# Router on the residual itself, routing in four batches, row numbers ahead of the weight splits, an early empty gather

## The chip, the core and the metric

One core of a Trainium2 chip runs the whole kernel. The metric is the device time of one execution in microseconds, the median of three runs. Five engines work from queues of their own: TensorE (PE; its weight loads are PEld), VectorE (DVE), ScalarE (ACT), GpSimd (POOL) and SyncE (SP, which here only issues transfers). DMA transfers are issued by SP, ACT and POOL.

## The reference

One layer on 1024 tokens of 1024 channels, float32. Only the last two residual steps are touched.

```python
x = x + mixed @ w_out
x = x + memory_cross_attention(x, mem, ...)          # 4 heads, 256 memory tokens
x = x + hierarchical_moe(rms_norm(x, norm_ffn), ...)

def rms_norm(x, g):
    return x * lax.rsqrt(jnp.mean(x * x, axis=-1, keepdims=True) + EPS) * g

def hierarchical_moe(hf, ...):                       # 4 groups x 8 experts
    gval, gidx = lax.top_k(softmax(hf @ w_group + b_group), 1)
    el = take_group(hf @ w_router + b_router, gidx)  # 8 logits of the chosen group
    ev, eidx = lax.top_k(el, 2)
    ew = softmax(ev) * gval
    # each expert: rows of hf sent to it, (silu(x @ w_g) * (x @ w_u)) @ w_down, times ew, added to out
```

## The kernel before, in words

Tokens come in 8 blocks of 128 (tb = 0 to 7). The kernel runs, in time: RMSNorm and the q, k, v and gate projections, differential attention, the RG-LRU, the merge and w_out, which leaves the residual in the tiles x1 (one per block); then the memory attention with the router, and last the 32 experts.

Every weight comes through the class `Weights` as pieces of 128 x 1024 floats (512 KB) that SP loads ahead. Each is split exactly into two parts of a shorter float format: ACT writes `wh` (L90), DVE writes `wl` (L94). Every product of large matrices is three matmuls on such parts (L152 to L154, `mm3`); `split` (L320, L321) does the same with activations, ACT first and then DVE. SBUF tiles come from one pool of 4-KB slots, so an instruction may also wait until the former holder of its slot is done. `prefetch` (op f) lets the stream run ahead by PF[i] pieces.

Between w_out and the experts, a string SEQ gives the order in which the steps are written. A letter is a step, a digit the block (or pair of blocks g):

- A, P, T, S: norm, query projection, its transposes, scores and softmax. O, M: transposes of the probabilities, product with the memory values (tile `om`, split by ACT, then DVE).
- C: product with w_co into `pco` (24 matmuls of 512 columns). It reads `om`.
- N (`st_N`): x1 += pco (DVE, L1007), squares with their sum (ACT, L1008), store of x1 to the output (issued by ACT, L1009), the row factor r = rstd on POOL (L1012 to L1014), then h3 = x1 * r * gain (DVE, L1018; tile `n`) and its store to DRAM, `h3_d` (issued by ACT, L1020). For blocks 6 and 7 the steps of N go in two halves.
- R (`st_R`): 8 transposes of h3 on PE (`ph3T`, L1033), split into `h3T`.
- L (`st_L`): router logits of a pair of blocks, 16 matmuls with the router weights as the stationary side (`plog`, 72 rows: a high and a low part of 36 logits, 256 tokens, L1045); bias and copy by ACT (`lgT`, L1049). l (`st_l`): transposes back and sum of the parts (`plgT`, L1055), copied by DVE (L1056).
- r and q (`st_route`): its first half chooses group and experts (some 25 small DVE operations, L1125 to L1143), its second half counts the rank of each token in its expert with matmuls (`prk`, L1147 to L1150) and builds one-hots (`ohs`, `vals`, L1167 and L1176). Batches are blocks 0-1, 2-3 and 4 to 7.

After SEQ, matmuls `pTi` and `pTw` (L1262) collect token numbers and weights per expert slot; DVE turns them into `idx` and `wts` (L1270 to L1272). POOL's indirect gather fetches the 96 rows of h3 of an expert from `h3_d` (tile `xe`, L1282); PE transposes them (`pxe`, L1292), and `pgu` begins the expert. An instruction scheduler orders each engine's queue within these steps; queues run in order.

Of the kernel before, what the change touches and what calls it, by code (L numbers as in the profile page):

```python
# [124 lines left out]
def block_kernel(ctx, tc, a):  # L125
# [301 lines left out]
    # --------------------------------------------------- differential attention  # L427
# [3 lines left out]
    def head_load(h):  # L431
        """Per map: q stacks its two parts on the partitions, k repeats each part."""
# [66 lines left out]
    def w_transpose(h, g):  # L499
        """Transposes of the query pair g; parts per two key blocks: [128 keys, 2, 256 queries]."""  # L500
# [141 lines left out]
    # ------------------------------------------------------------------ RG-LRU  # L642
# [17 lines left out]
    V.scalar_tensor_tensor(t5, t5, 2.0, t0, op0=OP.mult, op1=OP.add)   # softplus(-lam)  # L660
# [48 lines left out]
    def lru_gate(c):  # L709
        """2 * gelu of the gate."""  # L710
# [12 lines left out]
    def lru_scan(c):  # L723
        """Block-diagonal gates, recurrence, times the gate."""
# [25 lines left out]
    # memory keys and values  # L750
# [87 lines left out]
    # --------------------------------- attention output, gated: 2 * sigmoid(g) * y  # L838
# [12 lines left out]
    # -------------------------------------------------- LRU output, merge, w_out  # L851
# [22 lines left out]
    # ------------------------------------------- memory attention, MoE input  # L874
# [9 lines left out]
    nc.sync.dma_start(wr, a["w_r"])  # L884
    A.activation(wrs[:, :, 0:36], wr, AF.Copy)
# [9 lines left out]
    def pair_T(src, kp, name):  # L895
        """Channels 256 * kp ... of two token blocks: parts [128 channels, 2 parts, 2, 256 tokens]."""
# [104 lines left out]
    def st_N(tb, ps):  # L1001
# [19 lines left out]
        x1[tb] = None  # L1021

    h3T, lgT = {}, {}

    def st_R(tb):
        """Transposes of a token block for the router: parts [128 channels, 4, 256 tokens]."""
        src = h3.pop(tb)
        c = slice((tb % 2) * P, (tb % 2) * P + P)
        for kq in range(2):
            ps = bank(f"ph3T{tb}_{kq}", F32, (P, 4, P))  # L1030
# [3 lines left out]
            if tb % 2 == 0:  # L1034
                h3T[tb // 2, kq] = [slot(f"h3T{tb}_{kq}_{i}", F32R, (P, 4, 256)) for i in range(2)]
            t = h3T[tb // 2, kq]
            split(ps, t[0][:, :, c], t[1][:, :, c])

    def st_L(g):
        """Router logits of two token blocks: [36 high and 36 low parts, 256 tokens]."""  # L1040
        pl = bank(f"plog{g}", F32, (P, 256))[0:72]
# [9 lines left out]
    def st_l(g):
        src = lgT.pop(g)
        pt = bank(f"plgT{g}", F32, (P, 2, 36))
        for j in range(2):
# [34 lines left out]
    lgf = rt("lg", NB * 36)  # L1089
# [3 lines left out]
    id2 = rt("id2", 36)[0:72]  # L1093
    V.tensor_tensor(id2, ident[0:72, 0:36], ident[0:72, 36:72], op=OP.add)
    coded = []

    def st_route(b0, n2):
        """Choices of n2 token blocks, then their ranks within the experts and dispatch codes."""
# [14 lines left out]
        def first_hot(v, mxv, n):  # L1113
            """One-hot of the first maximum along the last axis."""
# [37 lines left out]
        # weights of the two choices  # L1152
        V.tensor_reduce(sg, gd, axis=AX.X, op=OP.add)
        V.reciprocal(gval, sg)
        V.tensor_tensor(m2, m2, m1, op=OP.subtract)
        A.activation(m2, m2, AF.Exp)
        V.tensor_scalar(dn, m2, 1.0, None, op0=OP.add)
        V.reciprocal(dn, dn)
        V.tensor_tensor(ew[:, 0, bs], dn, gval, op=OP.mult)
        V.tensor_tensor(ew[:, 1, bs], ew[:, 0, bs], m2, op=OP.mult)  # L1160
        V.tensor_copy(ewh[:, :, bs], ew[:, :, bs])
        V.tensor_tensor(ewl[:, :, bs], ew[:, :, bs], f(ewh[:, :, bs]), op=OP.subtract)
# [43 lines left out]
    PF = 12,20,28,36,41  # L1206
    SEQ = ("P0 T0 P1 T1 S0 S1 P2 P3 O00 O01 O02 T2 O03 T3 M00 M01 C0 A2 S2 S3 N0 C1 N1 P4 O10 O11 P5 "
# [3 lines left out]
    done = set()  # L1211
    routes = [st_route(0, 2), st_route(2, 2), st_route(4, 4)]
    pco = {}
    for op in SEQ.split():
# [29 lines left out]
        elif kind == "l":  # L1244
            st_l(n)
# [10 lines left out]
    def b3(ap, n):      # [P, NB] -> [P, NB, n]  # L1256
# [246 lines left out]
```

## Time and profile before

| what | value |
|---|---|
| median of 3 runs | 1965.66 us (1961.47, 1965.66, 1966.36) |
| profiled execution: span from first to last instruction | 1957.1 us |
| lowest run less that span | 4.4 us |
| median less that span | 8.6 us |
| PE busy | 1882.8 us, 96% |
| PEld, DVE, ACT, POOL busy | 79%, 66%, 56%, 17% |
| mean granted clock of TensorE | 0.988 |

The profiled execution is one of its own; only its span is known, and 4.4 to 8.6 us lie around it if it was like the timed runs. Busy shares are means over stages with different limits, so the stage that a change touches has to be read by itself. A row of the timeline gives the start, the duration (of the whole group if xN), engine, line, operation, output<-inputs, shapes, and in brackets the engine's idle time just before and what ended it.

### The profile page before, as it was taken

To read this page: it belongs to the slowest core of one execution; us is meant where nothing else is said; L and a number is where in the kernel's file an instruction comes from. 1 tells how busy PE (TensorE), PEld (TensorE's weight loads), DVE (VectorE), ACT (ScalarE), POOL (GpSimd) and SP (SyncE) were. 2 spreads that over 40 slices of the span, in tenths; PEclk is the share of its full clock that TensorE was granted. 3 is DMA by queue.
4 is the path that set the end of the run, shared out by engine and by line. 5 is a ranking of instruction groups with operands and counts; after the bars stand their busy time and mean duration, and the time that the engine had idled before them with its cause. 6 is when DMAs were issued, how large, how long until landed. Compare 5 with 4: busy or idle time off the path is not lost. (4 is left out here: it accounts for less than half of the span.)

```text
span 1957.1 us, 27981 instructions
## 1 busy us (share of the span) xinstructions
PE 1882.8 (96%) x10366; PEld 1551.2 (79%) x10366; DVE 1295.3 (66%) x1766; ACT 1087.6 (56%) x1607; POOL 337.1 (17%) x430
## 2 busy tenths in 40 slices
PE   7999999999999999989999999996999999999996
PEld 7999998888888888867888888885777777777664
DVE  5222233777778767887534434776899999999985
ACT  5222223555555545875412214543788888888885
POOL 2343251122222221110000000211111111111110
PEclk9999999999999999989999999998999999999998
DMA  4222225433334322214422511167999999999996
GB/s 167 98 80 94 87 87 152 133 99 115 96 108 120 107 81 79 82 51 173 150 67 84 197 33 65 54 248 296 297 340 361 345 349 360 340 354 342 352 368 217
DMA packets 103130, 353.53 MB, mean 181 GB/s; under 512 B 14224, under 2 KB 15376, under 8 KB 102992
## 3 DMA queue, kind: packets, MB, share of 16 engines
q1 hardware_dynamic: 91088, 322.10, 46.7%
q0 software_dynamic: 7296, 17.04, 3.8%
q10 hardware_dynamic: 4608, 12.58, 1.6%
q8 instruction: 82, 1.34, 0.3%
q14 instruction: 56, 0.46, 0.1%
HBM read 311.82 MB, written 48.23 MB: 184 GB/s over the span
## 5 line engine op out<-in xcount | busy, mean ns | idle before, releaser
L94 DVE TENSOR_TENSOR wl<-wraw,wh 128x1024 fp32r<-128x1024 f32 x480 | 578.4, 1230 | 104.2 <-ACT wh L90 91.9
L90 ACT ACTIVATE wh<-wraw 128x1024 fp32r<-128x1024 f32 x480 | 496.4, 1057 | 111.3 <-DVE wl L94 18.3
L153 PE MATMUL pgu<-wl,xeh 128*96 128x512 f32 x512 | 203.5, 397 | 1.2 <-DVE wl L94 1.0
L152 PE MATMUL pgu<-wh,xeh 128*96 128x512 f32 x512 | 203.4, 397 | 0.3 <-ACT wh L90 0.3
L154 PE MATMUL pgu<-wh,xel 128*96 128x512 f32 x512 | 200.9, 392 | 0.0
L486 ACT ACTIVATE p<-pS,st 128x256 f32<-128x256 f32 (+7 forms) x128 | 94.9, 747 | 93.7 <-DVE st L479 53.2
L154 PE MATMUL pqk<-wh,hL 128*128 128x256 f32 x512 | 145.2, 284 | 0.0
L153 PE MATMUL pqk<-wl,hH 128*128 128x256 f32 x512 | 145.1, 283 | 0.0
L152 PE MATMUL pqk<-wh,hH 128*128 128x256 f32 x512 | 145.0, 283 | 0.0
L152 PE MATMUL pga<-hH,wh 128*128 128x512 f32 x320 | 127.8, 399 | 3.5 <-DVE wT L520 3.5
L153 PE MATMUL pga<-hL,wh 128*128 128x512 f32 x320 | 126.3, 395 | 0.0
L154 PE MATMUL pga<-hH,wl 128*128 128x512 f32 x320 | 125.9, 393 | 0.0
L153 PEld LDWEIGHTS pgu<-wl,xeh 128*96 128x96 f32 x512 | 82.8, 162 | 44.0 <-DVE wl L94 13.0
L152 PEld LDWEIGHTS pgu<-wh,xeh 128*96 128x96 f32 x512 | 82.8, 162 | 33.8 <-ACT wh L90 0.5
L154 PEld LDWEIGHTS pgu<-wh,xel 128*96 128x96 f32 x512 | 82.8, 162 | 33.1 <-DVE xel L321 0.2
L1332 POOL DMA_INDIRECT out<-y,idx x32 | 46.5, 1453 | 357.2 <-ACT y L1331 352.6
L495 POOL TENSOR_SCALAR p<-p,st 128x128 f32<-128x128 f32 (+3 forms) x64 | 55.9, 873 | 294.4 <-DVE st L494 203.4
L153 PE MATMUL py<-wl,ah 128*96 128x512 f32 x256 | 101.8, 398 | 0.5 <-DVE wl L94 0.5
L154 PE MATMUL py<-wh,ah 128*96 128x512 f32 x256 | 100.5, 392 | 0.0
L152 PEld LDWEIGHTS pqk<-wh,hH 128*128 128x128 f32 x512 | 98.2, 192 | 0.0
L153 PEld LDWEIGHTS pqk<-wl,hH 128*128 128x128 f32 x512 | 98.2, 192 | 0.0
L154 PEld LDWEIGHTS pqk<-wh,hL 128*128 128x128 f32 x512 | 98.2, 192 | 0.0
(517 smaller groups left out, 4571.1 us busy)
## 6 DMA issues: line engine op xcount, KB each, us to landing
wraw<-in_w_gu SPq DMA_DIRECT2D x256, 512.0 KB
wraw<-in_w_dn SPq DMA_DIRECT2D x128, 512.0 KB
wraw<-in_w_cm SPq DMA_DIRECT2D x32, 512.0 KB
x<-in_x SPq DMA_DIRECT2D x16, 512.0 KB
wraw<-in_w_qk SPq DMA_DIRECT2D x16, 512.0 KB
qk_d<-qk SPq DMA_DIRECT2D x16, 512.0 KB
qr<-qk_d SPq DMA_DIRECT2D x32, 256.0 KB
kr<-qk_d SPq DMA_DIRECT2D x32, 256.0 KB
```

The source lines that it names most:

```text
L90: ins = nc.scalar.activation(h, raw, AF.Copy)
L94: nc.vector.tensor_sub(l, raw, h.bitcast(F32))
L152: W.seen(E.matmul(out, lh, rh, start=start, stop=False))
L153: E.matmul(out, lh, rl, start=False, stop=False)
L154: E.matmul(out, ll, rh, start=False, stop=stop)
L486: A.activation(p[:, :n], ps[:, :n], AF.Exp, bias=mx[:, m:m + 1], accum_out=ls[:, m:m + 1])
L495: G.tensor_scalar(pp[1][:, :n], pp[1][:, :n], rl[:, 1:2], 0.0, op0=OP.mult, op1=OP.add)
L1332: G.indirect_dma_start(out=a["out"][:, :], out_offset=bass.IndirectOffsetOnAxis(ap=dest, axis=0), in_=y, in_offset=None, bounds_check=T - ...
```

## The change

1. The router works on x1 instead of h3. R transposes x1 (`pxT`, tile `xT`); the router weights are multiplied once by the norm gain (`gcol`, loaded at the start by POOL as 1024 single floats). L takes one block: 16 matmuls with `xT` (128 x 128) as the stationary side and 72 columns of router weights moving, so the logits come token-major and the transposes back (l) are gone. Two DVE operations apply the row factor r3 and add the bias row and the two parts.
2. h3 = x1 * r3 * gain and its store become a step of their own, H.
3. Routing goes in four batches of two blocks, and within a batch codes, ranks and one-hots come before the weights.
4. `idx` comes ahead of the weight splits of the first expert (`W.anchor`).
5. An indirect gather with all row numbers out of bounds (tile `nil`) runs on POOL before the memory attention.
6. PF[3] is 33 instead of 36; SEQ is new.

```diff
+    gcol = cp.tile([P, 8], F32, name="gcol")
+        nc.gpsimd.dma_start(gcol, a["nffn"].rearrange("o (k p) -> p (o k)", p=P))
...
+    V.tensor_tensor(wr, wr, gcol[:, :, None].to_broadcast([P, 8, 36]), op=OP.mult)
...
-        for c in parts:
-            V.scalar_tensor_tensor(t[:, c], x[:, c], r[:, 0:1], gffn[:, c], op0=OP.mult, op1=OP.mult)
+            V.tensor_copy(r3[:, tb:tb + 1], r[:, 0:1])
         h3[tb] = t
+    def st_H(tb):
+        t = h3.pop(tb)
+        V.scalar_tensor_tensor(t, x1[tb], r3[:, tb:tb + 1], gffn, op0=OP.mult, op1=OP.mult)
         nc.scalar.dma_start(h3_d[tb * P:(tb + 1) * P, :], t)
...
-                W.last = E.matmul(pl, wrs[:, k, :], t[i][:, k % 4, :], start=k + i == 0, stop=k + i == 8)
+                W.last = E.matmul(pl, t[:, i, k % 4, :], wrs[:, k, :], start=k + i == 0, stop=k + i == 8)
...
-        A.activation(lgT[g], pl, AF.Identity, bias=vec[0:72, C_BR:C_BR + 1])
...
-            W.last = E.matmul(pt[:, j, :], src[:, j * P:(j + 1) * P], id2, start=True, stop=True)
-        V.tensor_copy(lg[:, 2 * g:2 * g + 2, :], pt)
+        V.scalar_tensor_tensor(lg[:, tb, :], pl[:, 0, :], r3[:, tb:tb + 1], brow, op0=OP.mult, op1=OP.add)
+        V.scalar_tensor_tensor(lg[:, tb, :], pl[:, 1, :], r3[:, tb:tb + 1], lg[:, tb, :], op0=OP.mult, op1=OP.add)
...
-    PF = 12,20,28,36,41
-    SEQ = ("P0 T0 P1 T1 S0 S1 P2 P3 O00 O01 O02 T2 O03 T3 M00 M01 C0 A2 S2 S3 N0 C1 N1 P4 O10 O11 P5 "
-           "O12 O13 T5 M10 M11 T4 A3 S5 R0 C2 R1 L0 S4 l0 r0 C3 N2 N3 P6 O20 O21 P7 T6 O22 O23 M21 f0 "
-           "f1 T7 S6 M20 q0 R2 S7 R3 O30 L1 C4 O32 N4 l1 r1 R4 O33 O31 C5 N5 f2 M31 M30 f3 C6 N6 R5 "
-           "L2 C7 N7 R6 f4 l2 R7 q1 L3 l3 r2 q2 ")
+    G.indirect_dma_start(out=nil, out_offset=None, in_=a["vec"][:, :],
+                         in_offset=bass.IndirectOffsetOnAxis(ap=idx[:, 0:1], axis=0), bounds_check=P - 1, oob_is_err=False)
+    PF = 12,20,28,33,41
+    SEQ = ("P0 T0 P1 T1 S0 S1 P2 P3 O00 O01 O02 T2 O03 T3 M00 M01 C0 A2 S2 S3 N0 C1 H0 N1 H1 P4 O10 O11 P5 "
+           "O12 O13 T5 M10 M11 T4 A3 S5 R0 C2 R1 L0 S4 L1 r0 C3 N2 H2 N3 H3 P6 O20 O21 P7 T6 O22 O23 M21 f0 "
+           "f1 T7 S6 M20 q0 R2 S7 R3 O30 L2 C4 O32 N4 H4 L3 r1 R4 O33 O31 C5 N5 H5 f2 M31 M30 f3 C6 L4 N6 R5 q1 "
+           "R6 L5 r2 C7 N7 q2 L6 R7 L7 r3 H6 H7 f4 q3 ")
-    routes = [st_route(0, 2), st_route(2, 2), st_route(4, 4)]
+    routes = [st_route(2 * i, 2) for i in range(4)]
...
-    table(pTi, pTw, wts, idx)
+    W.anchor, W.want = table(pTi, pTw, wts, idx), False
```

The diff moves instructions in the engines' queues. Three places matter.

ACT's queue between the squares of block 5 and the splits of `om3`, which C6 reads. `n3_5` is the tile of squares and then of h3, `om3_1` and `om3_0` are the two halves of the attention output of blocks 6 and 7. Before:

```order
790 L1008 ACTIVATE n3_5_11944,n3_5s_11945<-x1_5_10055 128x1024
791 L320 ACTIVATE om3_1_11984<-pmo3_1_11971 128x512
792 L320 ACTIVATE om3_0_12000<-pmo3_0_11987 128x512
793 L1020 DMA h3_d_10020<-n3_5_11944 128x1024
794 L320 ACTIVATE h3T4_0_0_11890<-ph3T5_0_12060 128x4x128
```

And with the change:

```order
787 L1013 ACTIVATE n3_5_11989,n3_5s_11990<-x1_5_10060 128x1024
788 L1014 DMA out<-x1_5_10060 128x1024
789 L1030 DMA h3_d_10022<-n3_5_11989 128x1024
790 L323 ACTIVATE om3_1_12030<-pmo3_1_12017 128x512
791 L323 ACTIVATE om3_0_12046<-pmo3_0_12033 128x512
```

The store of h3 of block 5 stood behind the two splits and now stands ahead of them.

PE's queue from the end of C6 (`pco6`) to the start of C7 (`pco7`). Before:

```order
7189 L154 MATMUL pco6_1_12020<-wh95_10931,om3_1_11984 128x512
7190 L1033 MATMUL ph3T5_1_12067<-ident_98,n3_5_11944 128x128 x4
7191 L1045 MATMUL plog2_12074<-h3T4_0_0_11890,wrs_10028 72x256
...
7198 L1045 MATMUL plog2_12074<-h3T4_0_1_11891,wrs_10028 72x256
7199 L152 MATMUL pco7_0_12093<-wh92_10658,om3_0_12000 128x512
```

With the change:

```order
7165 L154 MATMUL pco6_1_12060<-wh95_10943,om3_1_12030 128x512
7166 L1048 MATMUL pxT5_0_12116<-ident_100,x1_5_10060 128x128 x4
7167 L1048 MATMUL pxT5_1_12124<-ident_100,x1_5_10060 128x128 x4
...
7176 L1048 MATMUL pxT6_0_12156<-ident_100,x1_6_10062 128x128 x4
7177 L1048 MATMUL pxT6_1_12164<-ident_100,x1_6_10062 128x128 x4
7178 L1060 MATMUL plog5_12172<-wrs_10030,xT5_0_12121 128x72 x8
7179 L1060 MATMUL plog5_12172<-wrs_10030,xT5_1_12129 128x72 x8
7180 L152 MATMUL pco7_0_12215<-wh92_10670,om3_0_12046 128x512
```

The transposes of blocks 5 and 6 and the logits of block 5 now stand between C6 and C7. The logits of block 4 (`plog4`, 16 matmuls) moved into C6, behind its fourth matmul.

ACT and DVE feed that stretch of PE. ACT's queue there, with the change:

```order
793 L1014 DMA out<-x1_6_10062 128x1024
794 L1013 ACTIVATE n3_6_12104,n3_6s_12105<-x1_6_10062 128x512 x2
795 L323 ACTIVATE xT5_0_12121<-pxT5_0_12116 128x512
796 L323 ACTIVATE xT5_1_12129<-pxT5_1_12124 128x512
797 L1030 DMA h3_d_10022<-n3_6_12104 128x1024
```

Where the splits of block 5's transposes before stood ahead of the squares of block 6, they now stand behind them, and so behind the end of C6.

DVE's queue around `idx`. Before:

```order
1202 L1176 TENSOR_TENSOR ohs4_12271<-im99_10032 128x384 x2
1203 L1167 TENSOR_TENSOR vals4_12270<-im99_10032 128x8x32
1204 L94 TENSOR_TENSOR wl96_12326<-wraw96_10929,wh96_12325 128x1024
1205 L94 TENSOR_TENSOR wl97_12330<-wraw97_10935,wh97_12329 128x1024
1206 L1270 TENSOR_SCALAR idx_12315<-pTi_12280 96x32
```

With the change:

```order
1261 L1166 TENSOR_TENSOR vals6_12386<-im99_10035 128x4x32
1262 L1287 TENSOR_SCALAR idx_10638<-pTi_12405 96x32
1263 L1288 COPY wts_12439<-pTw_12406 96x32
1264 L1289 TENSOR_TENSOR wts_12439<-wts_12439,pTw_12406 96x32
1265 L94 TENSOR_TENSOR wl96_12450<-wraw96_10941,wh96_12449 128x1024
```

The two weight splits ahead of `idx` are gone from there.

## Rows read from the trace of the kernel before

**Rows 1.** The page's first line.
```profile
span 1957.1 us, 27981 instructions
```

**Rows 2.** Windows: stretch; busy us of PE, PEld, DVE, ACT, POOL; clock, DMA share, GB/s.
```profile
1345.00:1372.00 27.00, 13.37 (x85) 11.45 (x84) 18.58 (x63) 7.80 (x12) 4.43 (x3) 0.63 0.52 204
1411.00:1835.00 424.00, 424.00 (x2014) 299.03 (x2013) 388.53 (x384) 364.05 (x431) 58.68 (x48) 1.00 1.00 348
```

**Rows 3.** Waits from 1830 us on: total, times, longest.
```profile
ACT wh L90 <- DMA wraw<-in_w_gu: 7.8, 15, 2.2
```

**Rows 4.** Timeline of PE, 1318 to 1372 us.
```profile
1320.15 0.39 PE L154 MATMUL pco<-wh,om 128*128 128x512 f32 x1
1320.39 1.04 PE L1033 MATMUL ph3T<-ident,n 128*128 128x128 f32 x8
1321.26 1.04 PE L965 MATMUL ppT<-ident,mp 128*128 128x128 f32 x8
...
1326.91 0.50 PE L152 MATMUL pco<-wh,om 128*128 128x512 f32 x1 [1.18 <-ACT om L320]
...
1333.32 1.17 PE L1045 MATMUL plog<-h3T,wrs 128*72 128x256 f32 x8
1334.33 0.39 PE L152 MATMUL pco<-wh,om 128*128 128x512 f32 x1
...
1340.54 0.40 PE L154 MATMUL pco<-wh,om 128*128 128x512 f32 x1
1342.56 1.23 PE L1033 MATMUL ph3T<-ident,n 128*128 128x128 f32 x8 [1.62 <-DVE n L1018]
...
1351.26 0.51 PE L1262 MATMUL pTw<-vals 128*96 128x64 f32 x4
1351.60 0.49 PE L1262 MATMUL pTi<-vals 128*96 128x32 f32 x4
...
1356.34 0.27 PE L1148 MATMUL prk<-mb,tri 128*128 128x128 bf16 x1 [3.90 <-DVE mb L1143]
...
1368.47 1.51 PE L1292 MATMUL pxe<-ident,xe 96*128 96x96 f32 x8 [7.02 <-DMA xe<-h_d,idx]
1369.92 0.74 PE L152 MATMUL pgu<-wh,xeh 128*96 128x512 f32 x1
```

**Rows 5.** Timeline of DVE, the same stretch.
```profile
1320.59 1.22 DVE L1007 TENSOR_TENSOR x<-x,pco 128x1024 f32<-128x1024 f32 x1
1325.36 1.28 DVE L1018 SCALAR_TENSOR_TENSOR n<-x,n_5r,gffn 128x1024 f32<-128x1024 f32 x1
...
1340.98 0.69 DVE L1007 TENSOR_TENSOR x<-x,pco 128x512 f32<-128x512 f32 x1 [3.01 <-PE pco L154]
...
1351.19 0.17 DVE L1125 TENSOR_REDUCE route<-im 128x4 f32<-128x16 f32 x1
...
1359.34 2.35 DVE L94 TENSOR_TENSOR wl<-wraw,wh 128x1024 fp32r<-128x1024 f32 x2
1361.61 0.18 DVE L1270 TENSOR_SCALAR idx<-pTi 96x32 int32<-96x32 f32 x1
```

**Rows 6.** Timeline of ACT, the same stretch (ACTq: issue of a transfer).
```profile
1323.24 1.07 ACT L1008 ACTIVATE n<-x 128x1024 f32<-128x1024 f32 x1
...
1325.78 1.09 ACT L320 ACTIVATE om<-pmo 128x512 fp32r<-128x512 f32 x2 [1.37 <-PE pmo L154]
1326.67 0.33 ACTq L1020 DMA_DIRECT2D h_d<-n  x1
```

**Rows 7.** Timeline of POOL, at the start and ahead of the memory attention.
```profile
5.60 0.18 POOL L221 TENSOR_SCALAR n_0m<-n_0s 128x1 f32<-128x1 f32 x1 [1.40 <-ACT n_0j L228]
...
1201.09 0.19 POOL L221 TENSOR_SCALAR rc0m<-ssc 128x4 f32<-128x4 f32 x1 [12.67 <-DVE ssc L924]
```

**Rows 8.** Chain that ended last, the first two gathers: start, duration, what.
```profile
1362.67 5.66 DMA xe<-h_d,idx
...
1370.26 5.15 DMA xe<-h_d,idx
```

More of the change, by code (lines that the diff above doesn't have):

```diff
@@ L205, in block_kernel @@
     nc.gpsimd.dma_start(row, a["row"].to_broadcast([P, NROW]))
+    gcol = cp.tile([P, 8], F32, name="gcol")
+    with nc.allow_non_contiguous_dma(reason="1024 gains, one per channel"):
+        nc.gpsimd.dma_start(gcol, a["nffn"].rearrange("o (k p) -> p (o k)", p=P))
     posi = cp.tile([P, NB], I32, name="posi")
@@ L1010, in st_N, with used @@
         if n == 2:
-            m, r = (sm.tile([P, 16], F32, tag=f"rs{i}", name=f"n3_{tb}r{i}") for i in range(2))
+            m = sm.tile([P, 16], F32, tag="rs0", name=f"n3_{tb}r0")
+            r = sm.tile([P, 16], F32, tag="rs1", name=f"n3_{tb}r1")
             G.tensor_scalar(ss[:, 0:1], ss[:, 0:1], 1.0, D * EPS, op0=OP.mult, op1=OP.add)
             G.tensor_scalar(m[:, 0:1], ss[:, 1:2], ss[:, 0:1], 1.0 / D, op0=OP.add, op1=OP.mult)
-            G.tensor_tensor(r[:, 0:1], m[:, 0:1], negh[:, 0:1], op=OP.pow)
+            G.tensor_tensor(r3[:, tb:tb + 1], m[:, 0:1], negh[:, 0:1], op=OP.pow)
         else:
             r = rstd_of(ss[:, 0:1], 1, D, f"n3_{tb}")
-        for c in parts:
-            V.scalar_tensor_tensor(t[:, c], x[:, c], r[:, 0:1], gffn[:, c], op0=OP.mult, op1=OP.mult)
+            V.tensor_copy(r3[:, tb:tb + 1], r[:, 0:1])
         h3[tb] = t
+    def st_H(tb):
+        t = h3.pop(tb)
+        V.scalar_tensor_tensor(t, x1[tb], r3[:, tb:tb + 1], gffn, op0=OP.mult, op1=OP.mult)
         nc.scalar.dma_start(h3_d[tb * P:(tb + 1) * P, :], t)
-        x1[tb] = None
-    h3T, lgT = {}, {}
+        used(tb)
+    xT, uses = {}, [0] * NB
+    def used(tb):
+        uses[tb] += 1
+        if uses[tb] == 2:
+            x1[tb] = None
     def st_R(tb):
-        src = h3.pop(tb)
-        c = slice((tb % 2) * P, (tb % 2) * P + P)
+        src = x1[tb]
         for kq in range(2):
-            ps = bank(f"ph3T{tb}_{kq}", F32, (P, 4, P))
+            ps = bank(f"pxT{tb}_{kq}", F32, (P, 4, P))
             for kk_ in range(4):
@@ L1033, in st_R, with st_L @@
                 E.transpose(ps[:, kk_, :], src[:, k * P:(k + 1) * P], ident)
[L1034 to L1041, printed above, removed]
+            t = xT[tb, kq] = slot(f"xT{tb}_{kq}", F32R, (P, 2, 4, P))
+            split(ps, t[:, 0], t[:, 1])
+        del src
+        used(tb)
+    def st_L(tb):
+        pl = bank(f"plog{tb}", F32, (P, 2, 36))
         for k in range(8):
-            t = h3T[g, k // 4]
+            t = xT[tb, k // 4]
             for i in range(2):
-                W.last = E.matmul(pl, wrs[:, k, :], t[i][:, k % 4, :], start=k + i == 0, stop=k + i == 8)
+                W.last = E.matmul(pl, t[:, i, k % 4, :], wrs[:, k, :], start=k + i == 0, stop=k + i == 8)
             if k % 4 == 3:
-                del h3T[g, k // 4]
-        lgT[g] = slot(f"lgT{g}", F32, (P, 256))[0:72]
-        A.activation(lgT[g], pl, AF.Identity, bias=vec[0:72, C_BR:C_BR + 1])
[L1051 to L1054, printed above, removed]
-            W.last = E.matmul(pt[:, j, :], src[:, j * P:(j + 1) * P], id2, start=True, stop=True)
-        V.tensor_copy(lg[:, 2 * g:2 * g + 2, :], pt)
+                del xT[tb, k // 4]
+        V.scalar_tensor_tensor(lg[:, tb, :], pl[:, 0, :], r3[:, tb:tb + 1], brow, op0=OP.mult, op1=OP.add)
+        V.scalar_tensor_tensor(lg[:, tb, :], pl[:, 1, :], r3[:, tb:tb + 1], lg[:, tb, :], op0=OP.mult, op1=OP.add)
     rpool = {}
@@ L1088, in block_kernel @@
     mb = cp.tile([P, NB, 32], BF, name="mb")
-    lgf = rt("lg", NB * 36)
+    lgf, brow, r3 = rt("lg", NB * 36), rt("brow", 36), rt("r3", NB)
+    pbr = bank("pbr")
+    E.transpose(pbr[:, 0:P], vec[:, C_BR:C_BR + 1].to_broadcast([P, P]), ident)
+    V.tensor_copy(brow, pbr[:, 0:36])
+    del pbr
     lg = lgf.rearrange("p (a b) -> p a b", a=NB)
@@ L1151, in st_route @@
                      start=False, stop=t == n2 - 2)
[L1153 to L1162, printed above, removed]
         va = rt(f"vals{b0}", 2, n2, 3, 32, dt=F32R)
@@ L1177, in st_route @@
                             rk[:, k, bs, None].to_broadcast([P, n2, CAP]), op=OP.is_equal)
+        V.tensor_reduce(sg, gd, axis=AX.X, op=OP.add)
+        V.reciprocal(gval, sg)
+        V.tensor_tensor(m2, m2, m1, op=OP.subtract)
+        A.activation(m2, m2, AF.Exp)
+        V.tensor_scalar(dn, m2, 1.0, None, op0=OP.add)
+        V.reciprocal(dn, dn)
+        V.tensor_tensor(ew[:, 0, bs], dn, gval, op=OP.mult)
+        V.tensor_tensor(ew[:, 1, bs], ew[:, 0, bs], m2, op=OP.mult)
+        V.tensor_copy(ewh[:, :, bs], ew[:, :, bs])
+        V.tensor_tensor(ewl[:, :, bs], ew[:, :, bs], f(ewh[:, :, bs]), op=OP.subtract)
         value(1, f(ewh))
@@ L1205, in block_kernel @@
     NG_ = NB // 2
-    PF = 12,20,28,36,41
-    SEQ = ("P0 T0 P1 T1 S0 S1 P2 P3 O00 O01 O02 T2 O03 T3 M00 M01 C0 A2 S2 S3 N0 C1 N1 P4 O10 O11 P5 "
[3 rows of a table removed]
+    idx = cp.tile([P, 32], I32, name="idx")[0:CAP]
+    V.memset(idx[:, 0:1], 2 * T)
+    nil = slot("nil", F32, (P, NVEC))[0:CAP]
+    G.memset(nil, 0.0)
+    G.indirect_dma_start(out=nil, out_offset=None, in_=a["vec"][:, :],
+                         in_offset=bass.IndirectOffsetOnAxis(ap=idx[:, 0:1], axis=0), bounds_check=P - 1, oob_is_err=False)
+    PF = 12,20,28,33,41
+    SEQ = ("P0 T0 P1 T1 S0 S1 P2 P3 O00 O01 O02 T2 O03 T3 M00 M01 C0 A2 S2 S3 N0 C1 H0 N1 H1 P4 O10 O11 P5 "
[3 rows of a table added]
     done = set()
-    routes = [st_route(0, 2), st_route(2, 2), st_route(4, 4)]
+    routes = [st_route(2 * i, 2) for i in range(4)]
     pco = {}
@@ L1243, in block_kernel @@
             st_L(n)
-        elif kind == "l":
-            st_l(n)
+        elif kind == "H":
+            st_H(n)
         elif kind == "w":
@@ L1268, in table @@
     def table(code, parts, w_, ix):
-        V.tensor_scalar(ix, code, 2.0 * T, None, op0=OP.add)
+        ins = V.tensor_scalar(ix, code, 2.0 * T, None, op0=OP.add)
         V.tensor_copy(w_, parts[:, 0])
         V.tensor_tensor(w_, w_, parts[:, 1], op=OP.add)
+        return ins
     wts = cp.tile([P, 32], F32, name="wts")[0:CAP]
-    idx = cp.tile([P, 32], I32, name="idx")[0:CAP]
-    table(pTi, pTw, wts, idx)
+    W.anchor, W.want = table(pTi, pTw, wts, idx), False
     xe = slot("xe")[0:CAP]
```

2 lines of the change are left out of this document (removed).

## The prediction, on record before the changed kernel ran

> **What bounds the kernel now.** The page comes first: one program of 1957.1 us from its first to its last instruction [rows 1]. The sum is made against that span; the median of the three runs is 8.6 us above it, the lowest 4.4 us, and I carry every difference over to the median.
>
> Then the windows [rows 2]. In the experts, 1411 to 1835 us, PE is busy all the time and so is the DMA (share 1.00, 348 GB/s). From 1830 us on, ACT's weight splits wait for weight pieces [rows 3]: the stream sets the end, PE is just beside it. Both hang on one event. The stream stands still once it is as many pieces ahead as it may be, and goes on when the first expert's matmuls free slots. So whether PE or the stream ends last, the experts move as one block with the first `pgu`, at 1369.92 [rows 4]. The change leaves the stream's order as it was, so the question is when that `pgu` starts.
>
> Then the timelines of the 50 us ahead of it [rows 4 to 8]. Until 1340.94 (last `pco` of C7: 1340.54 + 0.40) PE runs nearly without gaps; its largest wait there is 1.18 us ahead of C6, for ACT's split of `om`. From then on a chain of small steps decides: C7's end to `idx` 20.67 us (1340.94 to 1361.61), `idx` to `pgu` 8.31 us. In 1345 to 1372 PE is busy half of the time and its mean granted clock 0.63 [rows 2].
>
> **The change part by part.** I follow the end of one step to the start of the next, before and after.
>
> *Price of L.* No row has 72 moving columns on 128 weight columns. The nearest: transposes with 128 by 128, eight in 0.87 us (1320.39 to 1321.26), 0.109 each; `pTw`, 96 weight columns and 64 moving, four in 0.34 (1351.26 to 1351.60), 0.085 each; `plog` itself with 256 moving, eight in 1.01 (1333.32 to 1334.33), 0.126 each [rows 4]. Sixteen cost 1.4 to 2.0; I take 1.9, near the transposes, plus the last one's tail. A pair of blocks costs 3.8 on PE against 2.0 for `plog` and some 0.4 for `plgT`: +1.4 per pair where PE is the bound.
> The Trainium skill ("TensorE: Matmul & The Clock Gate", Back-to-back issue gap) gives about 81 ns for matmuls of 128 columns in a row; the transposes here take 109. By the page an L would cost 1.3 us and the sum below would come out some 2 to 3 us lower.
>
> *Up to the end of C5: +3.8.* L0 and L1 lie in a stretch with some gaps: +0.6. L2 and L3 now stand ahead of C5's end where `plog1` and `plgT1` stood: +1.4. Sixteen transposes (block 4's and two of the probabilities), which followed C5 at 1320.39 to 1322.1, now come ahead of its end: +1.8.
>
> *C5's end to C6's start: +0.3.* Before: 1320.54 to 1326.91, 6.37, most of it PE work. That work has moved ahead, so the split of `om` could come soon. But in ACT's queue the store of `n3_5` now stands ahead of both `om` splits, and it waits for H5: x1 += pco 1.22 [rows 5]; start of the squares to h3, over POOL's row factor, 2.12 (1323.24 to 1325.36) [rows 5, 6]; a copy of the factor 0.2; h3 1.28; issue 0.33; two splits 1.09 [rows 6]; some 0.4 between engines. 6.6 in all, of which PE stands idle nearly 4.
> The Trainium skill ("DMA: Bandwidth & Descriptors", Anatomy of one DMA — SWDGE (gpsimd) path) says that the DMA engines never wait on semaphores: a wait is made by the issuing sequencer before dispatch. This speaks against putting that store there; no row of before shows ACT held by a store alone.
>
> *C6's start to C7's start: +8.5.* Before 7.42 (1326.91 to 1334.33): 24 matmuls, 8 transposes, 8 logits. After: the 24 matmuls take 5.5 (7.42 less 0.87 for the transposes and 1.01 for the logits), 16 logits 1.9, to C6's end. The clock: the idle 3.90 at 1352 lies in the stretch of mean clock 0.63, the idle 1.18 ahead of C6 does not; nearly 4 us idle ahead of C6 I price at 1.3 (bounds 0 and 7.4, all of C6 at the lower level, 1.2 GHz; near the low end, since C6 is solid matmul work, in which the rows of the experts show 1.00). From C6's end PE waits for this chain: x1 += half, 0.7; issue of the store of x1, 0.35; two squares of half a block, 1.3, which stand ahead of the splits of block 5's transposes; ACT split 0.55, DVE split 0.7, eight logits 0.95; then `xT5_1`, whose slot comes free with those eight: again 0.55, 0.7 and 0.95; waits between engines 0.5. 7.2. H6 (1.28) sits on DVE between the two splits, beside logits and ACT split (1.5): no cost. 5.5 + 1.9 + 1.3 + 7.2 = 15.9.
>
> *C7: -1.0.* The eight logits within it are gone.
>
> *C7's end to `idx`: -4.3.* Before 20.67, after 16.4: x1 += half, squares, row factor and H7 on DVE 3.9; behind it rests of the third batch's routing and two splits of `xT7`, 3.2; eight logits and two operations for r3 and bias, 1.4; choices of two blocks, 4.8 (four took 5.15, 1351.19 to 1356.34, and the operations are nearly as long with half the elements); `mb` to `idx` 3.1 where it took 5.3 (1356.3 to 1361.61), since two weight splits (2.35 [rows 5]) and half of the one-hots and `pTi` are off it.
>
> *`idx` to `pgu`: -1.0.* The first gather takes 5.66 and its start 1.06 after `idx`; the second 5.15 [rows 8]. If the early empty gather warms it, 0.5 to 1.5; never run empty in this trace.
>
> *At no cost.* The empty gather: before `rc0m` POOL is idle for 12.67 us. `gcol` on POOL at the start: idle 1.40 ahead of `n_0m` [rows 7] covers it; if 1024 single floats take longer to issue than that, the start moves by 0 to 3. Other H on DVE: PE is the bound there. PF[3]: pieces that come later are needed 33 pieces on.
>
> Sum: 3.8 + 0.3 + 8.5 - 1.0 - 4.3 - 1.0 = +6.3. 1965.7 + 6.3 = 1972.0 us, span about 1963.4.
>
> **The rivals.** A difference under 0.3% (5.9 us) is about what a measurement of this kernel can't tell from no change.
>
> *Small loss, within 0.3%.* L at its low end (1.4: 2 to 3 us less on the path), or the clock holds (1.3 less), or the waits ahead of C7 hide in one another. +1 to +5: 1967 to 1971. All the terms are near their middles, so this is nearly as likely as the forecast.
>
> *Gain.* The store does not hold the `om` splits, and the splits of block 5 come ahead of the squares in time: PE runs from C5 to C7 without the two waits, 2.6 and 7.2 less. Then +6.3 - 9.8 = -3.5, and with a gather at its best and L at its low end -7: 1958.5 to 1962. It decides from the point where ACT's queue is empty when C6 ends. For it: ACT is mostly idle around C6 [rows 6]. Against it: the order of ACT's queue, as shown above. By the page on DMA it can't come about for the store.
>
> *Larger loss.* The low clock lasts through C6 and until C7 (3 more), `gcol` delays the start (up to 3), or pieces of the stream that come after the last logits collide with the first gather (1 more): +9 to +13, 1975 to 1979.
>
> *The experts swallow the shift.* If the end were set by the stream alone and the stream ran through the gap, a later `pgu` would cost nothing: 1965. Against it: the stream stops at its bound before `pgu` (DMA share 0.52 in 1345 to 1372, 1.00 in the experts [rows 2]).
>
> **How the numbers follow.** Forecast, +5.9 to +9: 0.40. Larger loss 0.10. Together slower by over 0.3%: 0.50. Small loss 0.35 and the swallowed shift 0.05 are within 0.3%; so is half of the gain, 0.05. The other half, 0.05, is faster by more. Same 0.45, faster 0.05. Range 1961 to 1978: it takes in the gain without its extremes, and most of the larger loss.
>
> **What would show it.** In the changed profile: ahead of C6's first `pco` an idle time of 3 to 4 us that ACT's `om` ends; `plog` with 72 columns at 0.11 to 0.12 apart; between C6 and C7 some 5 us of PE idle, ended by `xT5`; C7's end near 1352; `idx` near 1369, and the first `pgu` near 1376; from there on the experts as before, 6 us later. C7 ending before 1345, or a `pgu` before 1370, would make the prediction wrong; so would a first gather of 4 us or less, or experts that take another time.

## The result, and the profile after

The changed kernel takes 1987.82 us (median; 1984.86 to 1991.31) against 1965.97 for the kernel before on the same chip: ratio 1.0117, interval 1.0101 to 1.0134. It is slower, as forecast, but by 21.9 us where +6.3 was forecast, and lies above the range. The two profiled executions are 25.6 us apart (1957.1 [rows 1] and this):

```profile
span 1982.7 us, 28165 instructions
```

Two parts of similar size make up the 25.6. The first `pgu` starts 14.6 us later (1384.48 against 1369.92 [rows 4]), and from it to the end 598.2 us pass instead of 587.2. The prediction had +6.3 and 0. The medians are 3.7 us less apart than these two executions; e1 below shows that the experts spread that much.

**Ahead of the first expert.** The timeline of PE after:

```profile
1281.52 4.05 PE L1060 MATMUL plog<-wrs,xT 128*128 128x72 f32 x32
...
1310.39 0.47 PE L152 MATMUL pco<-wh,om 128*128 128x512 f32 x1
...
1328.05 0.39 PE L154 MATMUL pco<-wh,om 128*128 128x512 f32 x1
...
1335.27 0.50 PE L152 MATMUL pco<-wh,om 128*128 128x512 f32 x1 [3.82 <-ACT om L323]
...
1336.71 3.46 PE L1060 MATMUL plog<-wrs,xT 128*128 128x72 f32 x16
1339.98 0.77 PE L154 MATMUL pco<-wh,om 128*128 128x512 f32 x1
...
1345.68 0.39 PE L154 MATMUL pco<-wh,om 128*128 128x512 f32 x1
...
1349.89 1.08 PE L1060 MATMUL plog<-wrs,xT 128*128 128x72 f32 x8 [1.68 <-DVE xT L324]
1351.66 0.30 PE L1060 MATMUL plog<-wrs,xT 128*128 128x72 f32 x1 [0.69 <-ACT xT L323]
1352.39 1.29 PE L1060 MATMUL plog<-wrs,xT 128*128 128x72 f32 x7 [0.42 <-DVE xT L324]
1353.48 0.77 PE L152 MATMUL pco<-wh,om 128*128 128x512 f32 x1
...
1360.15 0.39 PE L154 MATMUL pco<-wh,om 128*128 128x512 f32 x1
...
1360.50 1.96 PE L1060 MATMUL plog<-wrs,xT 128*128 128x72 f32 x16
...
1384.48 0.74 PE L152 MATMUL pgu<-wh,xeh 128*96 128x512 f32 x1
```

The `pco` rows are the first or last of C4, C5, C6, C7. Step by step, in us:

| stretch | before | after | difference | forecast |
|---|---|---|---|---|
| to C4's start | 1305.49 | 1310.39 | +4.9 | +0.6 |
| C4's start to C5's end | 15.05 | 18.05 | +3.0 | +3.2 |
| C5's end to C6's start | 6.37 | 6.83 | +0.5 | +0.3 |
| C6's start to C7's start | 7.42 | 18.21 | +10.8 | +8.5 |
| C7 | 6.61 | 7.06 | +0.5 | -1.0 |
| C7's end to `idx` | 20.67 | 17.05 | -3.6 | -4.3 |
| `idx` to `pgu` | 8.31 | 6.89 | -1.4 | -1.0 |

The stop ahead of C6 came as told. ACT's queue has the store of `n3_5` in front of `om`, and that store waits for H5 on DVE:

```profile
1333.70 0.33 ACTq L1030 DMA_DIRECT2D h_d<-n  x1
1334.13 1.08 ACT L323 ACTIVATE om<-pmo 128x512 fp32r<-128x512 f32 x2 [2.95 <-DVE route L1129]
```
```profile
1332.38 1.28 DVE L1029 SCALAR_TENSOR_TENSOR n<-x,im,gffn 128x1024 f32<-128x1024 f32 x1
```

What else became slower is in the windows (columns as in [rows 2], the granted clock third from the end). TensorE ran at the lower of its two levels, 1.2 GHz, for parts of C6, C7 and the tail, and also from the last matmuls of L0 and L1 on (1284.6 us), where PE had no gap at all:

```profile
1281.00:1284.60 3.60, 3.60 (x33) 3.48 (x31) 2.22 (x4) 1.24 (x3) 0.00 (x0) 1.00 0.22 89
1284.60:1288.10 3.50, 3.50 (x13) 2.94 (x13) 2.18 (x13) 1.17 (x3) 1.48 (x4) 0.51 0.99 328
...
1335.00:1346.10 11.10, 10.83 (x42) 9.31 (x43) 3.14 (x11) 0.30 (x2) 0.00 (x0) 0.69 1.02 414
...
1353.00:1360.60 7.60, 7.60 (x33) 6.08 (x33) 4.56 (x20) 1.91 (x5) 0.19 (x1) 0.78 0.03 10
```

**Long before that.** POOL takes 0.98 us to issue `gcol`, and the idle time of `n_0m` shrinks from 1.40 [rows 7] to 0.59. From there on ACT's weight splits run 1.2 us late (the fifth starts at 54.38 us, at 53.20 before).

```profile
2.08 0.98 POOL L208 DMA_DIRECT2D gcol<-in_nffn  x1
...
5.70 0.18 POOL L224 TENSOR_SCALAR n_0m<-n_0s 128x1 f32<-128x1 f32 x1 [0.59 <-ACT n_0j L231]
```

In the product with w_out PE has two waits of a kind that the kernel before does not have there (waits between 1095 and 1112 us):

```profile
PE pwo L152 <- ACT wh L90: 0.6, 1, 0.6
PE pwo L153 <- DVE wl L94: 0.5, 1, 0.5
```

**In the experts** PE is as busy as before, but the stream delivers less. Packets and bytes from 1430 to 1785 us, first before, then after; q1 is SP's queue, its last column the share of the time of 16 DMA engines:

```profile
DMA packets 35724, 124.49 MB, mean 351 GB/s; under 512 B 5390, under 2 KB 5390, under 8 KB 35697
q1 hardware_dynamic: 31211, 113.66, 86.6%
```
```profile
DMA packets 34716, 120.90 MB, mean 341 GB/s; under 512 B 5258, under 2 KB 5258, under 8 KB 34688
q1 hardware_dynamic: 30208, 110.00, 85.7%
```

The engines are full in both (share 1.00 and 0.99 with all queues). A packet of q1 costs 0.866 x 355 x 16 / 31211 = 157.6 ns of an engine before and 161.1 after, 2.2% more in these two executions.

The loss does not show at once. In this window ACT splits 240 pieces in both kernels, while q1 brings 113.66 / 0.524 = 217 pieces before and 210 after; the rest comes out of the lead that the stream has built up. So the first 20 experts keep time: from the first `pgu` to that of the 21st expert 350.1 us pass before and 350.3 after. Only when the lead is used up do the two part, and the 27th expert begins after 456.4 and 463.6 us. From 1830 us on ACT waits longer for pieces. Beside the 7.8 us for `w_gu` [rows 3] before has 5.4, 13.2 in all; after has 19.4:

```profile
ACT wh L90 <- DMA wraw<-in_w_dn: 5.4, 6, 1.8
```
```profile
ACT wh L90 <- DMA wraw<-in_w_dn: 13.4, 15, 3.0
ACT wh L90 <- DMA wraw<-in_w_gu: 6.0, 14, 1.2
```

### The profile page after: what moved, and what is told of

Read it like the earlier page. It is cut to its first block, busy times and chain, and to the rows that moved or that the text cites. A ratio compares the mean times of both kernels' runs of the same rounds, so it can differ in the third digit from the quotient of the medians.

```text
span 1982.7 us, 28165 instructions
## 1 busy us (share of the span) xinstructions
PE 1902.0 (96%) x10421; PEld 1563.4 (79%) x10421; DVE 1305.3 (66%) x1823; ACT 1086.8 (55%) x1605; POOL 335.5 (17%) x433
## 4 chain that ended last, share of the span: by engine, by line
PE 54%; issue 18%; DMA 14%; DVE 8%; ACT 5%; POOL 1%; SPq 0%; POOLq 0%; ACTq 0%; DVEq 0%
DMA out<-y,idx 13%; PE pqk L154 3%; PE pqk L153 3%; PE pqk L152 3%; PE pga L152 3%; PE pga L153 3%; PE pga L154 3%; PE pv L154 2%; PE pv L152 2%; PE pv L153 2%; PE pya L153 1%; PE pya L154 1%; PE pyr L153 1%; PE pyr L154 1%; PE pyr L152 1%
```

## The experiments

Positions in SBUF below are those that the program's allocation gives, not a reading of the profile. In all kernels the weight stream fills slots of 4 KB. One thing of the change was not in the prediction at all: the 32-byte tile `gcol` pushes all of them from byte 19200 of a partition to 19232.

**e1: the changed kernel once more.** The line added is a comment.

> The changed kernel once more, unaltered. In its first profile the first pgu came 14.6 us later than before, and the time from there to the end was 598.2 us instead of 587.2. Theory A, the slower weight stream (1.69 us per piece instead of 1.65 in the middle of the experts) belongs to the program: pgu at 1384 to 1385, 596 to 600 us from there to the end, ratio 1.011. Rival B, the rate of the stream varies between executions or chips whatever the program: pgu at 1384 to 1385, but the rest anywhere from 587 to 600, and the kernel before varies as much on the same chip.

1987.35 us, ratio 1.0130 (1.0108 to 1.0153). First `pgu` at 1384.24, 593.0 us from there. So the first part repeats to 0.3 us, while the experts of one kernel differ by some 5 us between executions: for them the medians decide.

**e2: `gcol` loaded later, product on POOL.**

```diff
-    gcol = cp.tile([P, 8], F32, name="gcol")
...
+    gcol = cp.tile([P, 8], F32, name="gcol")          # beside the load of wr
-    V.tensor_tensor(wr, wr, gcol[:, :, None].to_broadcast([P, 8, 36]), op=OP.mult)
+    G.tensor_tensor(wr, wr, gcol[:, :, None].to_broadcast([P, 8, 36]), op=OP.mult)
```

> The changed kernel, but the column of gains is loaded by SP beside the router weights instead of by POOL at the start, and POOL instead of DVE multiplies the router weights by it. Theory: the load at the start costs 1.2 us and the product, late in DVE's queue, 1.6 us (ACT's copy of the router weights waits 1.92 us for it, and the weight splits behind it wait too). Then pgu comes 2.8 us earlier than in the changed kernel, at 1381.7, and PE waits neither at 1107 nor 1109 us. Rival: the 1024 single floats delay the weight pieces on SP's queue as much, and nothing is won.

The load stayed on POOL's queue, only behind other work; it did not go to SP. The 1.2 us at the start are gone: the fifth split starts at 52.52. How much of that `gcol` is, stays loose: with its load up front (after, e1, e3, e6) that split is 0.6 to 1.2 late, without it (e2, e4, e5, e7, e9 to e12) between 0.7 early and 0.7 late. Both waits at 1107 stay at 0.6 and 0.5, however, though ACT no longer waits for the product. That the product makes them has fallen. `pgu` came at 1385.96 instead of 1381.7, ratio 1.0123 (1.0092 to 1.0154): what was won was lost again to longer half clock, 6.8 us instead of 3.4 from 1282.6 us on (+1.6 up to C4), and around C6 and C7 (+1.8).

**e3: block 5's transposes ahead of C6, C7 ahead of L5 and R6.**

```diff
-  ... C5 N5 H5 f2 M31 M30 f3 C6 L4 N6 R5 q1 R6 L5 r2 C7 N7 q2 L6 R7 L7 r3 H6 H7 f4 q3
+  ... C5 N5 f2 M31 M30 f3 R5 C6 L4 H5 q1 N6 C7 L5 R6 N7 r2 L6 q2 R7 L7 r3 H6 H7 f4 q3
```

> The changed kernel with another order of the last steps: block 5's router transposes stand ahead of C6, and C7 ahead of the logits of block 5 and the transposes of block 6. The h3 store of block 5 still stands ahead of the splits of om. Theory: of the 18.2 us from C6's start to C7's start, the 7.4 us from C6's end to C7's start are a wait for ACT and DVE, and go; the clock stays up in C7; the work that stood between C6 and C7 (some 4 us of PE) comes behind C7, where PE waits anyway. pgu 6 to 9 us earlier than in the changed kernel, 1376 to 1379. Rival: the chain of block 6 and 7 behind C7 grows by as much as the gap shrinks, and pgu moves by under 2 us.

```profile
1336.04 0.47 PE L152 MATMUL pco<-wh,om 128*128 128x512 f32 x1 [3.42 <-DVE om L324]
...
1345.81 0.47 PE L152 MATMUL pco<-wh,om 128*128 128x512 f32 x1 [0.58 <-DVE route L1172]
```

C6 to C7 falls from 18.21 to 9.77, and C7 runs at full clock in 5.7. But C7's end to `idx` grows from 17.05 to 21.8, since L5, R6 and L6 are now there. Of 9.8 us saved in C6, C7 and between them, 4.2 arrive at `pgu` (1380.24), less than the theory's 6 to 9 and more than the rival's 2. Ratio 1.0092 (1.0060 to 1.0124). The wait ahead of C6 did not move with H5's place in the string; the scheduler put its store ahead of `om` again.

**e4: the kernel before with `idx` ahead of the splits and the empty gather.**

> The kernel before with two parts of the change alone: the row numbers ahead of the weight splits, and the early empty gather. Theory: idx comes 1.4 to 2.1 us earlier, the first gather is 1.0 to 1.5 us shorter, pgu at 1366.5 to 1367.5 instead of 1369.9, the experts as before: 1963. Rival C: the empty gather (or the earlier one) is what slows the weight stream in the experts; then from pgu to the end it takes 595 to 600 us and the time is 1971 or more.

C7's end to `idx` 18.82 (-1.9), `idx` to `pgu` 7.12 (-1.2), 583.5 us from `pgu` on, ratio .9997 (.9984 to 1.0010). Both parts do what they should, the stream takes no harm, and 3 us are too few to be told from no change. `pgu` came at 1368.90, later than the theory's 1366.5 to 1367.5: in the profiled execution an early stretch of half clock (6.8 us from 334 us on, 3.4 before) took 2 us back.

**e5 to e8 and e12: where the slots begin.** e5 is the kernel before with one unused tile. e6 is the changed kernel with `gcol` allocated behind the slots, all orders kept. e7, e8 and e12 are the kernel before with small tiles moved out from ahead of the slots (64, 256 and 128 bytes).

```diff
+    pad = cp.tile([P, 8], F32, name="pad")                    # e5
+    nc.vector.memset(pad, 0.0)
...
-    gcol = cp.tile([P, 8], F32, name="gcol")                  # e6
+    gcol = sm.tile([P, 8], F32, name="gcol", bufs=1)
...
-    negh = cp.tile([P, 16], F32, name="negh")                 # e7
+    negh = sm.tile([P, 16], F32, name="negh", bufs=1)
...
-    wts = cp.tile([P, 32], F32, name="wts")[0:CAP]            # e8 and e12
+    wts = lgf[0:CAP, 128:160]
-    idx = cp.tile([P, 32], I32, name="idx")[0:CAP]            # e8 alone
+    idx = lgf[0:CAP, 160:192].bitcast(I32)
```

> The kernel before with one unused tile of 8 floats (32 bytes) among the constants, set to zero once by DVE. It moves the base of the 51 slots of 4 KB, into which every weight piece lands, from 19200 to 19232 bytes, so from a multiple of 64 to 32 beyond one; all else stays in its order. In the changed kernel the tile gcol, also 32 bytes, does the same. Theory A1, the stream is slower because its slots lie off a multiple of 64 bytes: first pgu at 1370 to 1372 as before, 596 to 604 us from there to the end instead of 584 to 591, median 8 to 10 us above the kernel before (ratio 1.004 to 1.005). Rival A2, the slower stream comes from something else in the change (the order of loads and gathers, the prefetch by 33 pieces): 584 to 591 us, ratio 1.000.

> The changed kernel with gcol moved into the pool that lies behind the slots, so that their base is 19200 again; every engine's order is that of the changed kernel. Theory A1: first pgu at 1384 to 1386 as in the changed kernel, 584 to 591 us from there to the end instead of 593 to 604, median about 1977. Rival A2: 593 to 604 us and 1987.

> The kernel before with the tile negh (64 bytes) moved into the pool behind the slots: their base is 19136, a multiple of 64 but not of 128. If A1 holds and 64 bytes are what matters: as before, 584 to 591 us from the first pgu to the end. If a multiple of 128 or 256 is wanted: longer, towards 600.

> The kernel before with idx and wts (256 bytes) laid into the logits tile, which is free by then: the base of the slots is 18944, a multiple of 512, where it was 256 beyond one. If more than 64 bytes count, the stream gets faster still: under 584 us from the first pgu to the end, and the time falls under 1960. If not: as before, ratio 1.000.

> The kernel before with one 128-byte tile (the weights per expert slot) taken from the tile of the logits instead of space of its own: all slots of the stream begin 128 bytes lower, 19072 bytes into a partition, a multiple of 128 and not of 256. So far the bases 19200 and 18944, multiples of 256, were fast, 19232 (32 over a multiple of 256) lost 0.65%, and 19136 (64 short of one) 0.27%. Theory A (only a base off a multiple of 64 or 128 costs time, the more the farther off): no loss, ratio .999 to 1.001. Theory B (a packet that does not begin at a multiple of 256 is cut in one piece more, wherever in the 256 bytes it begins): a loss as with the other two, ratio 1.002 to 1.007, the first expert's matmuls as in the kernel before (1369 to 1371) and 591 to 597 us from there to the end. The Trainium skill (DMA: Bandwidth & Descriptors, How a descriptor splits into AXI transactions) gives the rule from which theory B is taken: descriptors are cut at addresses that are multiples of 256 bytes.

| kernel | slots begin at | over a multiple of 256 | 90% of the stream's 4-KB packets within (1430 to 1785 us) | first `pgu` to end, profile | ratio to before |
|---|---|---|---|---|---|
| before | 19200 | 0 | 198.5 ns | 587.2 us | 1 |
| e8 | 18944 | 0 | 199 | 592.7 | 1.0005 (.9993 to 1.0018) |
| e12 | 19072 | 128 | 205 | 591.7 | 1.0020 (1.0007 to 1.0033) |
| e7 | 19136 | 192 | 213 | 591.8 | 1.0027 (1.0013 to 1.0042) |
| e5 | 19232 | 32 | 209 | 596.5 | 1.0065 (1.0048 to 1.0082) |
| after | 19232 | 32 | 215 | 598.2 | 1.0117 (1.0101 to 1.0134) |
| e6 | 19200 | 0 | 198 | 589.6 | 1.0070 (1.0048 to 1.0091) |

The median packet lasts 159 ns in all of them; only the upper end moves. Over all fourteen profiles the 90% mark parts the two kinds: 194 to 199 ns in the seven with a base at a multiple of 256, 204 to 225 in the seven with another. The same window as above, first of e5, then of e6:

```profile
q1 hardware_dynamic: 30585, 111.39, 85.7%
```
```profile
q1 hardware_dynamic: 31019, 112.96, 86.4%
```

An unused tile of 32 bytes makes the kernel before 0.65% slower, and its removal from ahead of the slots makes the changed one 10 us faster (1976.99). This part of the loss is shown from both sides, and rival A2 falls. That ACT and VectorE, which read the same slots, become slower by the position was another way to lose the time; the traces rule it out, since their weight splits last 1056 and 1222 ns in the mean in this window, before and after as well as in e5 and e6. e7 shows that a multiple of 64 is not enough, and e8 that 256 bytes further down nothing is gained. e8 shows that single executions spread (592.7 at an undisturbed base), so its ratio counts. e12 speaks for a cost at any place off a multiple of 256, though its interval begins close to 1 and the size differs with the place. The Trainium skill ("DMA: Bandwidth & Descriptors", How a descriptor splits into AXI transactions) says that descriptors are cut at multiples of 256 bytes, so that one of 4 KB that starts elsewhere makes a piece more. The five bases agree with it in sign; it gives no reason why 32 costs more than 128 or 192, and no run here shows one.

**e9: the places mended together.** `gcol` late and behind the slots, product on POOL, order of e3, and two more edits:

```diff
-    pbr = bank("pbr")
+    pbr = bank2("pbr")
...
-        nc.scalar.dma_start(h3_d[tb * P:(tb + 1) * P, :], t)
+        d = nc.scalar.dma_start(h3_d[tb * P:(tb + 1) * P, :], t)
+        if tb == 5:
+            W.after(d, om_ins[3, 0])      # ACT's split of om3_0, order only
```

> The changed kernel with five places mended at once: the gains' tile lies behind the slots (their base as in the kernel before), its load stands late and the product is made on GpSimd; the bias row's transpose takes a two-bank PSUM tile instead of one of the four one-bank tiles; block 5's transposes stand ahead of C6; C7 stands ahead of block 5's logits and block 6's transposes; the store of block 5's row waits in ACT's queue until the split of om3_0 has been issued. All arithmetic of the change stays. Theory (the loss is the sum of these places and of the longer stretches at half clock that the router's matmuls and the idle time bring): no wait of PE for ACT's or VectorE's weight parts in pwo0 near 1107, C4 starts at most 3.5 us later than in the kernel before, PE idles at most 1.5 us ahead of C6, C6 and C7 run at full clock, the first expert's matmuls start between 1370 and 1375 us, 590 +- 4 us from there to the end, median 1960 to 1967. Rival A (the sixteen added transposes and the 128 router matmuls of 72 columns cost what they last, wherever they stand): the first expert's matmuls start between 1377 and 1381 (C4 +4.9, C5 +3.0, less 2 to 5 in the tail), median 1969 to 1974. Rival B (the bias row's bank was not what PE waited for at 1107): the two waits of .59 and .48 us stay there, and 1.6 us of the early loss with them.

Both waits at 1107 are gone, and C4 starts at 1305.44, as in the kernel before. Late load, product on POOL and the base alone had left them (e2, e6). So the early waits hung on the transposed bias row: by the program it holds one of the four one-bank PSUM tiles until DVE has copied it, and `pwo` has one block less to work on with the first weight piece. (Rival B falls.) After the same 32 matmuls of L0 and L1 the clock stayed at 1.00. But ahead of C6 PE still waits:

```profile
1330.23 0.47 PE L152 MATMUL pco<-wh,om 128*128 128x512 f32 x1 [2.92 <-DVE im L1191]
```
```profile
1327.27 1.28 DVE L1031 SCALAR_TENSOR_TENSOR n<-x,im,gffn 128x1024 f32<-128x1024 f32 x1
...
1329.40 0.68 DVE L321 TENSOR_TENSOR om<-pmo,om 128x512 fp32r<-128x512 f32 x1
1330.00 0.15 DVE L1191 TENSOR_TENSOR im<-im,ewh 128x4 f32<-128x4 f32 x1
1330.07 0.68 DVE L321 TENSOR_TENSOR om<-pmo,om 128x512 fp32r<-128x512 f32 x1
```

ACT had split `om` by 1327.7. Now DVE's half of the split is late, behind H5 itself and seven routing operations. The store was one of two things in front of `om`, each of which was enough. 3.4 us of half clock follow in C6. `pgu` at 1374.39, 589.7 us from there, 1969.19 us, ratio 1.0037 (1.0023 to 1.0052). The `pgu` is as the theory had it, so rival A falls too; the wait ahead of C6 and the clock in C6 are not, and the median lies 2 us above it.

**e10: the kernel before with the whole tail of the change**, four batches of choices too.

> The kernel before with the change's tail alone: choices in four batches of two blocks (codes ahead of the weights of the choices), row numbers ahead of the weight splits, the early empty gather; the router as before. Theory: with the router behind block 7's normalised rows, the last two batches stand one behind the other on VectorE, some twenty short instructions more between the last copy of logits and the row numbers, so that C7's end to the row numbers is 19.5 to 21.5 us (20.67 before, 18.82 with one last batch of four blocks), the first expert's matmuls start at 1368 to 1371, ratio .999 to 1.001. Rival (smaller batches shorten the end because only two blocks' choices are left when the last logits land): 17.0 to 18.3 us, as in the changed kernel (17.05), and a ratio of .997 to .999, the first version that beats the kernel before.

`idx` 21.56 us after C7's end (e4: 18.82), `pgu` at 1369.39, ratio 1.0014 (.9995 to 1.0032). Small batches bring nothing where the last two must both follow the last blocks: they end 5.9 us apart on DVE. The rival falls.

**e11: `om` first on DVE too.** e9 with the choices of blocks 2 and 3 and H5 behind the split of `om3_0`.

```diff
+            W.after(hm, om_ins[3, 0][1])       # H5's product behind DVE's split
...
-  ... L3 r1 R4 O33 O31 C5 N5 f2 M31 M30 f3 R5 C6 ...
+  ... L3 R4 O33 O31 C5 N5 f2 M31 M30 r1 f3 R5 C6 ...
```

> The kernel of e9 with one more move: the last router batch that stood ahead of C6 (choices of blocks 2 and 3) and block 5's normalised row follow the split of om3_0 on VectorE too, not its store on ACT alone. In e9 ACT had both om splits done by 1327.7, but VectorE made its parts only at 1329.4 to 1330.8, behind that row (1.28 us) and some ten routing operations, and PE stood idle for 2.92 us. Theory (the wait ahead of C6 comes from what stands in front of om on both engines' queues, the store and the row itself): PE idle ahead of C6 0.8 to 1.6 us, C6 starts 1.3 to 2.2 us earlier counted from C5's end, C6 at full clock, the first expert's matmuls between 1370.5 and 1373 us, 587 to 591 us from there to the end, ratio .999 to 1.003. Rival (the idle time moves on: the batch that is later now holds the ranks' matmuls ahead of C7, or half clock comes all the same): C6 starts earlier, but the wait ahead of C7 grows from 0.58 to 2 us or more, the first expert's matmuls again between 1373.5 and 1375.5, ratio 1.003 to 1.005.

```profile
1329.76 0.47 PE L152 MATMUL pco<-wh,om 128*128 128x512 f32 x1 [0.62 <-DVE om L321]
...
1337.95 0.47 PE L152 MATMUL pco<-wh,om 128*128 128x512 f32 x1 [0.58 <-DVE route L1178]
...
1372.69 0.74 PE L152 MATMUL pgu<-wh,xeh 128*96 128x512 f32 x1
```

The idle time ahead of C6 is 0.62, C5's end to C6's start 4.36 instead of 6.67, C6 takes 5.8 at full clock, and the wait ahead of C7 did not grow. 1964.9 us, ratio 1.0004 (.9989 to 1.0019). With the arithmetic of the change untouched, the loss is gone within the interval: 1.0130 (e1), 1.0070 (base), 1.0037 (e9), 1.0004 (e11). No version here beats the kernel before by what a measurement can tell.

## Why the prediction was wrong

**"The experts move as one block ... The change leaves the stream's order as it was."** This step failed, and it is the larger part of the miss. The order is the same, and the first 20 experts did keep time with the first `pgu`; the rate of the stream is not the same, and 11 us were lost after its lead was used up. The sum asked of each new tile what work it costs and never where it lies. e5 and e6 put 10 to 13 us of the medians on the base of the slots. The rule that the stream sets the end [rows 2, 3] was right there and should have led to the question what the stream itself depends on. Experts that take another time were one of the prediction's own signs of being wrong.

**"L0 and L1 lie in a stretch with some gaps: +0.6" and "`gcol` ... covers it".** The shift at C4 was +4.9: start 1.2, `pbr`'s bank 1.75 (the shift at C0 is 2.93; in e1 and e2 as much less their own start, 1.74 and 1.67), L0 and L1 0.36, half clock after them 1.63 (from C0's start to C4's 78.58 us pass before, 78.94 in e9 without half clock there, 80.57 in the changed kernel). So 0.6 for the work of L0 and L1 was enough; the other three were missing. For `gcol` the bound of 0 to 3 held; the value taken, nothing, is a little low, and e2 leaves its size between 0 and 1.2. The bias row's PSUM tile was not priced at all, because its work was short; what counts is how long it holds the bank.

**The clock, 1.3 in C6 and nothing elsewhere.** C6 took 10.8 us, of which 24 matmuls at full clock are 5.5 and the logits 1.9; the other 3.4 are what half clock cost. C7 lost 1.4 to it (7.06; 5.7 in e9, all at full clock). Solid matmul work after the gap was no protection; the bound of 7.4 showed that the price was open. The rival of a larger loss, at 0.10, named the clock and `gcol`; the clock came, but without the base and the bank its +13 was too little.

**Right.** C4 to C5 (+3.0 for +3.2), the store that holds `om` (idle 3.82 for "nearly 4"), C6's end to C7's start (7.41 for 7.2, though with 2.8 us of idle time in it where some 5 were told: PE's own transposes and logits took more of it), the tail (-3.6 for -4.3), the gather: 4.31 us in the chain where [rows 8] has 5.66.

```profile
1378.58 4.31 DMA xe<-h_d,idx
```

An L took 1.96 us at full clock (16 in the rows at 1360.50) for 1.9. The Trainium skill ("TensorE: Matmul & The Clock Gate", Back-to-back issue gap) gives 81 ns for matmuls of 128 columns; these of 72 columns take 0.12 each (1.96 / 16), so the measured rows were the better guide. What the explanation of the store lacked is shown by e9: H5 and the routing in front of it on DVE alone hold `om` nearly as long (2.92).

## What to carry to other kernels

Before a small constant is added, look at what its bytes push: a stream that is the bound can lose more by the position of its buffers than the constant's work costs, and an unused tile tests it in one run. When an operation is taken away from one queue's head, look at the other engine that does the second half of the same split; the wait is over only when both are free. A short-lived PSUM tile is priced by how long it holds its bank while the neighbours want it.

## Not expected of the hardware

With a destination 32 bytes further on, packets of the stream became slower at the upper end alone: 90% of those of 4 KB are within 198.5 ns before, 209 (e5) and 215 (after) with it, the median is 159 in all three. The mean of one execution shows it less surely. A packet of q1 cost 1.0% more of an engine in e5 (0.857 x 355 x 16 / 30585 = 159.2 ns) and 2.2% in the changed kernel, but e8, at a multiple of 256, stands at 160.2 too.

TensorE went to half clock at 1284.6 us, with the last four of 32 gap-free matmuls of 72 columns, and stayed there for 3.4 us, mostly of matmuls of 512 columns, again without a gap; so it is in e1, e3 and e6, and in e2 for 6.8 us. e11, with the same 32 matmuls, shows 1.00 there, and so does e9, whose row this is:

```profile
1282.00:1288.80 6.80, 6.80 (x36) 5.71 (x35) 5.71 (x25) 1.81 (x6) 0.83 (x3) 1.00 0.82 311
```

What decides this is open.
